# A two-layer SSD and HGRN2 trunk in float32: the SSD layer's TensorE order written out by hand, with one run of 64-wide products a tile, the time steps spread over 128 partitions, products of zeros at the start, another place for the residual's load, and new amounts of background work in HGRN

## The chip, the cores and the metric

The kernel runs on one core of a Trainium2 chip. The metric is the device time of one execution in microseconds (us), the median of several runs. TensorE (PE) multiplies matrices, VectorE (DVE) and ScalarE (ACT) work on elements, GpSimd (POOL) does almost nothing here, and the queue of SyncE (SP) issues all DMA transfers.

## The reference, cut to what matters

One sequence of 512 tokens with 1024 features passes two layers. Layer 0 mixes tokens with Mamba-2 SSD, layer 1 with HGRN2; each is followed by a layer norm, a squared-ReLU MLP, a second norm and a gated embedding. The part that the change rewrites most is the SSD mixer (32 heads of 64 columns in 4 groups, state 128, chunks of 128 tokens):

```python
zxbcdt = u @ w_in
z, xbc, dt = jnp.split(zxbcdt, [SSD_D_INNER, SSD_D_INNER + SSD_CONV_DIM], axis=-1)
xbc = jax.nn.silu(causal_depthwise_conv(xbc, conv_w, conv_b))
...
dt = jax.nn.softplus(dt.astype(jnp.float32) + dt_bias.astype(jnp.float32))
...
xdt = xs * dt[..., None]
a_cs = jnp.cumsum(da, axis=2)
cb = jnp.einsum('bclgn,bcsgn->bcgls', cm, bm)
y_diag = jnp.einsum('bcgls,bcgrls,bcsgrp->bclgrp', cb, decay, xdt)
decay_to_end = jnp.exp(a_cs[:, :, -1:] - a_cs)
states = jnp.einsum('bclgn,bclgr,bclgrp->bcgrpn', bm, decay_to_end, xdt)
...
y_off = jnp.einsum('bclgn,bcgrpn,bclgr->bclgrp', cm, prev, jnp.exp(a_cs))
y = y_diag + y_off + d_skip.astype(jnp.float32).reshape(g_, r_)[:, :, None] * xs
y = y.reshape(bsz, seq, SSD_D_INNER) * jax.nn.silu(z.astype(jnp.float32))
y = rms_norm(y.reshape(bsz, seq, g_, SSD_D_INNER // g_), norm_w.reshape(g_, SSD_D_INNER // g_))
```

## The kernel before, in words

Large products are made of three: both operands are split into a high part and a rest, and `mm3` (L114) multiplies high by high, high by low and low by high (L115 to L117). A weight tile (`unit`, L98) is loaded by SP into one of three `raw` buffers; ACT rounds it to its high part (L109) and DVE subtracts (L111).

**The start.** Eight DMAs bring x and the first four weight tiles together (`slots`, the first four in the memory of the residual `acc`). PE runs eight k-steps of four tiles each, twelve products a step. After step 3 it takes in the dt projection (L499): eight 32-wide products of 512 columns, spread over four groups of rows that DVE adds afterwards (L508, L510). DVE and ACT then work out softplus, the decay and its running sum on 32 partitions of 512 columns (L512 to L541). `dt_tail` turns three results to tokens on partitions. The residual x is loaded into `acc` (L711) when its slots have been read, and scaled (L713).

**SSD.** Tile j of 16 holds a pair of heads. `xz(j)` projects its x and z (24 products each) and runs the convolution (four steps: ACT L557, DVE L560 three times) and silu. `core(j)` transposes x (L619), multiplies by dt and by the weights to the chunk's end, forms three state products (L631), sums them over chunks on DVE (`pv`, L638 to L641), builds the masked decay `m` (L647 to L651), then the eight diagonal products (L661, 64 columns wide, one for each head and chunk) and three off-diagonal ones (L666, 128 wide), whose result DVE multiplies by the decay `ecs` and adds (L674, L675). Every four tiles the group's rms (L691) and output projection follow. The code is written with `core` one tile behind `xz`; the framework's scheduler decides by priorities which engine does what when, so PE's order mixes products of different tiles. PSUM has four banks `pj` for projections and one each for `pt`, `py0`, `py1` and `pm`.

**HGRN.** Here PE's order is written by hand: four pairs of heads pass nine stages, and between stages a generator of background work (the other projections and half of the output projection) is drawn on for an amount of `FILL`, after `AHEAD` at the start. An amount of 0.68 stands for three products of 512 columns. `need` draws on it without counting when a pair's q, f, v or g isn't there yet. The stage `gates` multiplies q by f on DVE (L872 to L874); the next product (L882, 80 columns) reads it. L965 to L969 prepare the operands of L990.

Of the kernel before, what the change touches and what calls it, by code (L numbers as in the profile page):

```python
# [11 lines left out]
AF = mybir.ActivationFunctionType  # L12
# [22 lines left out]
FILL = dict(gates=3.0, first=7.0, fours=5.5, halves=5.0, blocks=4.0, turn=2.7, state=4.0, out=6.7, end=3.0)  # L35
AHEAD = 3.0
# [4 lines left out]
def trunk(ctx: ExitStack, tc, a):  # L41
# [28 lines left out]
    two = dict(xs=2, sz=2, cv=2, cm=2, cbm=2)  # L70
    mlp = dict(r=8, blk=2, sg=2)
    bufs = dict(ssd=dict(two, ss=2), mlp0=mlp, hgrn=dict(qx=2, f=2, k=4, qo=2, qt=2, xc=2, gg=2, tot=2, sc=2, scd=2, btok=2, pv=2), mlp1=mlp)
# [70 lines left out]

    x_s = Split(8)
# [28 lines left out]
    dtc = cols["dtc"][0:32]  # L173
    cmask = tmp("cm", [32, T])
    nc.gpsimd.memset(cmask, 1.0)
    nc.gpsimd.memset(cmask.rearrange("p (c l) -> p c l", c=NCH)[:, :, 0:1], 0.0)
# [318 lines left out]
    for k in range(8):  # L495
        if k == 4:
            for i in range(8):
                r = 32 * (i % 4)
                nc.tensor.matmul(  # L499
                    ps[r : r + 32], dtw[:, 32 * i : 32 * i + 32], slots[i][:, 0, :], start=i < 4, stop=i >= 4  # L500
                )
        for i, out in enumerate(first):
            hi, lo = (v[:, k % 2, i * P : (i + 1) * P] for v in four[k // 2])
            mm3(out, hi, lo, x_s.h(k), x_s.l(k), k == 0, k == 7)
    row = lambda tag: tmp(tag, [32, T])
    dtb, alog = dtc[:, 0:1], dtc[:, 1:2]
    pre = row("pv")
    nc.vector.tensor_copy(pre, ps[0:32])  # L508
    for r in (32, 64, 96):
        nc.vector.tensor_add(pre, ps[r : r + 32], pre)  # L510
# [16 lines left out]
    ea = mk(cpool, [32, 1], "ea")  # L527
# [4 lines left out]
    nc.vector.tensor_tensor_scan(cs, cmask, da, 0.0, ALU.mult, ALU.add)  # L532
    csd = a["csd"]
    nc.sync.dma_start(csd, cs)

    wt = row("sz")
    csv = cs.rearrange("p (c l) -> p c l", c=NCH)
    last_cs = cs.rearrange("p (c l) -> p c l", c=NCH)[:, :, P - 1]
    nc.vector.tensor_sub(wt.rearrange("p (c l) -> p c l", c=NCH), bc(last_cs, 2, P), csv)
    nc.scalar.activation(wt, wt, AF.Exp)  # L540
    nc.vector.tensor_mul(wt, wt, dt)  # L541
    def dt_tail():

        toks = []
        for src, tag in ((dt, "dt_tok"), (wt, "w_tok"), (cs, "cs_tok")):
            pt = bank(pst, "pt")
            for c in range(NCH):
                nc.tensor.transpose(pt[:, c * 32 : (c + 1) * 32], src[:, c * P : (c + 1) * P], ident[:32, :32])
            t = mk(cpool, [P, NCH, 32], tag)
            nc.vector.tensor_copy(t, pt[:, : 4 * 32].rearrange("p (c h) -> p c h", c=NCH))  # L550
            toks.append(t)
        return toks
# [29 lines left out]
    def bc_prep(bcm):  # L582
        bm, cm = bcm
        pt = bank(pst, "pt")
# [4 lines left out]
        pc = bank(psy, "py0")  # L589
# [9 lines left out]
    toks = []  # L599

    def xz(j):
        ps = projected(10 * (j // 4) + 2 + 2 * (j % 4))
        xs = tmp("xs", [P, T])
        conv_silu(ps, j, xs)
        if j == 1:
            toks.extend(dt_tail())
# [3 lines left out]
        return xs, sz  # L610

    def core(j, xs, sz, y, toks, btok, cbm, cm):
        dt_tok, w_tok, cs_tok = toks
# [3 lines left out]
        pt = bank(pst, "pt")  # L617
        for c in range(NCH):
            nc.tensor.transpose(pt[:, c * P : (c + 1) * P], xs[:, c * P : (c + 1) * P], ident)  # L619
        xdt = tmp("xdt", [P, 8, 64])  # L620
        v = pt.rearrange("p (c h q) -> p (c h) q", c=NCH, h=2)
        xdt4 = xdt.rearrange("p (c h) q -> p c h q", c=NCH)
        hs = slice(2 * j, 2 * j + 2)
        ptv = pt.rearrange("p (c h q) -> p c h q", c=NCH, h=2)
        nc.vector.tensor_mul(xdt4, ptv, bc(dt_tok[:, :, hs], 3, 64))
        xw = tmp("xw", [P, 3, 2, 64])
        nc.vector.tensor_mul(xw, ptv[:, 0:3], bc(w_tok[:, 0:3, hs], 3, 64))

        pst_ = bank(psm, "pm")
        for c in range(3):  # L630
            nc.tensor.matmul(  # L631
                pst_[:, c * P : (c + 1) * P], btok[:, c, :], xw[:, c].rearrange("p h q -> p (h q)"), start=True, stop=True
            )
        cd = mk(sm, [P, 2, NCH], "cd")
        nc.scalar.activation(cd, csb.rearrange("p h (c l) -> p h c l", c=NCH)[:, :, :, P - 1], AF.Exp)
        pv = tmp("pv", [P, 3, 2, 64])
        stv = pst_[:, : 3 * P].rearrange("p (c h q) -> p c h q", c=3, h=2)
        nc.vector.tensor_copy(pv[:, 0], stv[:, 0])  # L638
        for c in range(1, 3):
            nc.vector.tensor_mul(pv[:, c], pv[:, c - 1], bc(cd[:, :, c], 2, 64))  # L640
            nc.vector.tensor_add(pv[:, c], stv[:, c], pv[:, c])  # L641

        m = mk(w4, [P, 2, T], "b")
        for r in range(2):
            for c in range(NCH):
# [11 lines left out]
        yd = bank(psy, "py0")  # L657
        for c in range(NCH):
            sl = slice(c * P, (c + 1) * P)
            for r in range(2):  # L660
# [17 lines left out]
    def sq_sum(y, ss):  # L678
        sq = tmp("ss" if ss is None else "sq", [P, T])
        nc.scalar.activation(sq, y, AF.Square)  # L680
        if ss is None:
            return sq
# [524 lines left out]
```

## Time and profile before

| | us |
|---|---|
| median of 3 runs | 1442.93 (1442.82 to 1443.78) |
| the profiled execution | 1443.15 |
| its span on the core | 1441.4 |
| SSD, first real product to first transposition for the norm | 4.85 to 370 |
| first MLP and gate, to HGRN's first 80-column product | 370 to 827 |
| HGRN's head pairs, to the last pair's output transposition | 827 to 1030 |

How to read the rows: a timeline row is start, length, engine, line, operation, output<-inputs, shapes, count, and in brackets the idle time before it with what ended it. Products in float32 (those not from `mm3`) leave two records each, transpositions one. A group's row has the total busy time, the mean in ns of one, and the idle time before.

### The profile page before, as it was taken

What the parts mean: (1) busy time and instruction counts of PE and PEld (TensorE: products, weight loads), DVE (VectorE), ACT (ScalarE), POOL (GpSimd) and SP (SyncE); (2) the same over time, 40 slices, a digit from 0 to 9 for tenths busy, and PEclk for the clock granted to TensorE, in tenths of its full rate; (3) what the DMA queues carried; (4) which work ended last, traced back from release to release, by engine and by line L of the source; (5) the groups of instructions that cost most, each with busy time, mean ns of one, the idle gap of its engine ahead of it and who ended that gap; (6) DMA issues with size and microseconds to landing.
All of it is one profiled execution on the core that took longest, in us unless ns stands there. A gap on an engine that the chain in (4) does not pass through costs nothing.

```text
span 1441.4 us, 20138 instructions
## 1 busy us (share of the span) xinstructions
PE 1422.9 (99%) x7992; PEld 1176.7 (82%) x7992; DVE 1042.7 (72%) x1729; ACT 734.7 (51%) x1080; POOL 1.9 (0%) x11
## 2 busy tenths in 40 slices
PE   8999999999999999999999999999999999999998
PEld 6788888888888888888888887887798888888887
DVE  7999677787966768677863557558795867667873
ACT  5886455554255454535542454645455454544541
POOL 0000000000000000000000000000000000000000
PEclk9999999999999999999999999999999999999999
DMA  6343333323433444443422322222433444444231
GB/s 257 123 139 121 112 109 103 104 100 103 175 117 121 145 135 155 133 149 114 146 89 75 117 89 75 88 89 65 156 118 117 137 142 146 139 139 161 88 118 44
DMA packets 48383, 174.82 MB, mean 121 GB/s; under 512 B 5376, under 2 KB 6016, under 8 KB 48160
## 3 DMA queue, kind: packets, MB, share of 16 engines
q1 hardware_dynamic: 48288, 173.52, 35.9%
q8 instruction: 63, 1.03, 0.3%
q14 instruction: 32, 0.26, 0.1%
HBM read 171.34 MB, written 2.16 MB: 120 GB/s over the span
## 4 chain that ended last, share of the span: by engine, by line
PE 91%; DVE 5%; ACT 2%; DMA 1%; issue 1%; SPq 0%; ACTq 0%
PE pj L115 23%; PE pj L116 23%; PE pj L117 23%; PE py L116 5%; PE py L117 5%; PE py L115 5%; PE py L661 1%; PE pm L631 1%; DVE wlo L111 1%; PE pt L224 1%; PE py L666 1%; DMA raw<-in_wssd 1%; PE pt L619 1%; PE py L882 1%; PE py L1027 0%
## 5 line engine op out<-in xcount | busy, mean ns | idle before, releaser
L109 ACT CAST whi<-raw 128x1024 fp32r<-128x1024 f32 x224 | 234.6, 1051 | 348.3 <-PE pj L116 217.7
L111 DVE TENSOR_TENSOR wlo<-raw,whi 128x1024 fp32r<-128x1024 f32 x224 | 272.0, 1219 | 158.7 <-ACT whi L109 154.3
L115 PE MATMUL pj<-b,whi 128*128 128x512 f32 (+1 forms) x1008 | 382.2, 380 | 0.7 <-ACT b L228 0.7
L116 PE MATMUL pj<-b,whi 128*128 128x512 f32 (+1 forms) x1008 | 381.1, 378 | 0.0
L117 PE MATMUL pj<-b,wlo 128*128 128x512 f32 (+1 forms) x1008 | 380.8, 378 | 0.2 <-DVE wlo L111 0.2
L115 PE MATMUL pj<-whi,b 128*128 128x512 f32 (+1 forms) x584 | 229.5, 393 | 0.7 <-ACT sg L478 0.5
L117 PE MATMUL pj<-whi,b 128*128 128x512 f32 (+1 forms) x592 | 230.0, 389 | 0.0
L116 PE MATMUL pj<-wlo,b 128*128 128x512 f32 (+1 forms) x584 | 227.4, 389 | 0.0
L117 PEld LDWEIGHTS pj<-b,wlo 128*128 128x128 f32 x1008 | 189.7, 188 | 34.7 <-DVE wlo L111 0.6
L116 PEld LDWEIGHTS pj<-b,whi 128*128 128x128 f32 x1008 | 189.9, 188 | 33.4 <-issue 1.0
L115 PEld LDWEIGHTS pj<-b,whi 128*128 128x128 f32 x1008 | 189.5, 188 | 33.4 <-ACT b L228 0.9
L117 PEld LDWEIGHTS pj<-whi,b 128*128 128x128 f32 x592 | 111.3, 188 | 22.4 <-issue 0.2
L115 PEld LDWEIGHTS pj<-whi,b 128*128 128x128 f32 x584 | 109.7, 188 | 23.7 <-ACT b L1068 0.7
L116 PEld LDWEIGHTS pj<-wlo,b 128*128 128x128 f32 x584 | 109.8, 188 | 21.0
L109 ACT CAST whi<-r 128x1024 fp32r<-128x1024 f32 x64 | 67.4, 1053 | 63.7 <-PE pj L117 35.6
L111 DVE TENSOR_TENSOR wlo<-r,whi 128x1024 fp32r<-128x1024 f32 x64 | 78.1, 1220 | 22.6 <-ACT whi L109 22.3
L117 PE MATMUL py<-whi,b 128*128 128x512 f32 x216 | 84.1, 389 | 0.0
L116 PE MATMUL py<-wlo,b 128*128 128x512 f32 x192 | 74.7, 389 | 0.0
L115 PE MATMUL py<-whi,b 128*128 128x512 f32 x192 | 74.4, 389 | 0.0
L560 DVE SCALAR_TENSOR_TENSOR cv<-pj,cst,cv 128x509 f32<-128x509 f32 (+2 forms) x66 | 49.0, 742 | 5.0 <-ACT cv L557 4.5
L117 PEld LDWEIGHTS py<-whi,b 128*128 128x128 f32 x216 | 40.5, 188 | 8.5
L115 PEld LDWEIGHTS py<-whi,b 128*128 128x128 f32 x192 | 36.0, 188 | 7.6
(293 smaller groups left out, 1829.7 us busy)
## 6 DMA issues: line engine op xcount, KB each, us to landing
raw<-in_w SPq DMA_DIRECT2D x112, 512.0 KB, 3.3
r<-in_w SPq DMA_DIRECT2D x64, 512.0 KB, 3.6
raw<-in_wssd SPq DMA_DIRECT2D x36, 512.0 KB, 3.4
a<-csd SPq DMA_DIRECT2D x16, 512.0 KB, 3.8
raw<-in_wso SPq DMA_DIRECT2D x16, 512.0 KB, 3.3
raw<-in_wg SPq DMA_DIRECT2D x16, 512.0 KB, 3.3
raw<-in_whvg SPq DMA_DIRECT2D x16, 512.0 KB, 3.4
raw<-in_whq SPq DMA_DIRECT2D x16, 512.0 KB, 3.3
```

The costliest lines, as they stand in the source:

```text
L109: nc.scalar.copy(hi[:, :n], f)
L111: nc.vector.tensor_sub(lo[:, :n], f, f32(hi[:, :n]))
L115: nc.tensor.matmul(out, sh, mh, start=start, stop=False, **kw)
L116: nc.tensor.matmul(out, sh, ml, start=False, stop=False, **kw)
L117: nc.tensor.matmul(out, sl, mh, start=False, stop=stop, **kw)
L224: nc.tensor.transpose(pt[:, j * P : (j + 1) * P], src[:, k * P : (k + 1) * P], ident)
L560: nc.vector.scalar_tensor_tensor(cv[:, d:], ps[:, : T - d], convw[:, i, k : k + 1], cv[:, d:], ALU.mult, ALU.add)
L619: nc.tensor.transpose(pt[:, c * P : (c + 1) * P], xs[:, c * P : (c + 1) * P], ident)
L631: nc.tensor.matmul(pst_[:, c * P : (c + 1) * P], btok[:, c, :], xw[:, c].rearrange("p h q -> p (h q)"), start=True, stop=True)
L661: nc.tensor.matmul(yd[64 * r : 64 * r + 64, sl], xdt[:, 2 * c + r, :], m[:, r, sl], start=True, stop=True)
L666: nc.tensor.matmul(yo[:, c * P : (c + 1) * P], pv[:, c - 1].rearrange("p h q -> p (h q)"), cm[:, c * P : (c + 1) * P], start=True, stop=True,)
L882: nc.tensor.matmul(ps[r][32 * b : 32 * b + 32, base + n * c : base + n * c + n], kk[r][:, ts], moving(r, 4 * c + b), start=True, stop=True,)
```

## The change

At the start PE multiplies a tile of zeros eight times; in k-step 0 the four high-by-high products stand first, then high weights' rests, then those with the low part of x. The dt projection is cut into 32 products of 128 columns, so that four groups of 32 partitions each hold one chunk; all steps on dt have 128x128 elements, the sum over four groups goes, and three transpositions take the place of twelve.

In SSD, PE's order is written by hand (`manual_schedule`): tile j's x projection, the states of tile j-1, the products of tile j-2, the z projection, the turning of x, and two parts of a finished group's output projection. `ecs` now holds the decay for both heads on all partitions and is multiplied by C before the product, so that the off-diagonal products are 64 wide too and add into the diagonal's bank. The residual's load and scaling stand in the code at tile 4 instead of 0. More buffers are given to seven tiles. In HGRN, `AHEAD` and six amounts change, and eight of the copies of the stage `blocks` move behind the turning of k.

```diff
-FILL = dict(gates=3.0, first=7.0, fours=5.5, halves=5.0, blocks=4.0, turn=2.7, state=4.0, out=6.7, end=3.0)
-AHEAD = 3.0
+FILL = dict(gates=2.0, first=7.0, fours=5.5, halves=4.5, blocks=4.5, turn=2.7, state=3.5, out=6.5, end=2.0)
+AHEAD = 20.0
...
+    zero = tmp("y", [P, P])
+    with tc.high_priority(offset=FIRST + 100):
+        nc.vector.memset(zero, 0.0)
+        rest = bank(psm, "pm")
+        for i in range(8):
+            nc.tensor.matmul(rest[:, 0:P], zero, zero, start=True, stop=True)
...
-                r = 32 * (i % 4)
-                nc.tensor.matmul(
-                    ps[r : r + 32], dtw[:, 32 * i : 32 * i + 32], slots[i][:, 0, :], start=i < 4, stop=i >= 4
-                )
+                for c in range(NCH):
+                    nc.tensor.matmul(
+                        ps[32 * c : 32 * c + 32, 0:P],
+                        dtw[:, 32 * i : 32 * i + 32],
+                        slots[i][:, 0, c * P : (c + 1) * P],
...
+        if k == 0:
+            for out, (hi, lo) in zip(first, parts):
+                nc.tensor.matmul(out, hi, x_s.h(0), start=True, stop=False)
+            for out, (hi, lo) in zip(first, parts):
+                nc.tensor.matmul(out, lo, x_s.h(0), start=False, stop=False)
+            for out, (hi, lo) in zip(first, parts):
+                nc.tensor.matmul(out, hi, x_s.l(0), start=False, stop=False)
...
-    row = lambda tag: tmp(tag, [32, T])
+    row = lambda tag: tmp(tag, [P, P])
...
-        ecs = tmp("ecs", [P, 3 * P])
-        for r in range(2):
-            rs = slice(64 * r, 64 * r + 64)
-            nc.scalar.activation(ecs[rs], csb[rs, r, P:], AF.Exp)
+        ecs = tmp("ecs", [P, 2, 3 * P])
+        nc.scalar.activation(ecs, csb[:, :, P:], AF.Exp)
+        nc.vector.tensor_mul(ecs, ecs, bc(cm[:, P:], 1, 2))
...
+    def mixed(j):
+        xs, sz, xw, xdt, cd, m, ecs, pv = live.pop(j)
+        yd = bank(psy, "py%d" % (j % 2))
+        for c in range(NCH):
+            sl = slice(c * P, (c + 1) * P)
+            for r in range(2):
+                nc.tensor.matmul(yd[64 * r : 64 * r + 64, sl], xdt[:, c, r, :], m[:, r, sl], start=True, stop=c == 0)
+            for r in range(2 if c else 0):
...
+                    pv[:, c - 1, r, :],
+                    ecs[:, r, (c - 1) * P : c * P],
...
+    with tc.manual_schedule(engines={mybir.EngineType.PE}):
+        for j in range(17):
+            if j < 16:
+                load_decay(j)
+                if j % 4 == 0:
+                    bcm[j // 4] = bc_group(j // 4)
+                x_part(j)
...
+            if j == 4:
+                nc.sync.dma_start(acc, a["x"])
+                for c in range(NCH):
+                    nc.vector.tensor_scalar(acc[:, c, :], acc[:, c, :], ALPHA, None, ALU.mult)
...
+            states(j - 1)
+            done = mixed(j - 2)
+            if j % 4 == 2 and j > 2:
+                outs = pieces(j // 4 - 1, rms_group(j // 4 - 1, bank(psy, "py1")))
+            finish(j - 2, *done)
+            if j < 16:
+                z_part(j)
...
+                turn_x(j, bank(pst, "pt"))
+                decays(j)
+                next(outs, None), next(outs, None)
```

What this does to the engines' orders is seen at three places. The first is PE's order around the products of tile 6, before the change:

```order
L115 MATMUL pj_1526<-b_3_100,whi_1529 128x512
L661 MATMUL py_264_1504<-b_1490,xdt_1474 64x128 x4
L631 MATMUL pm_1478<-xw_1476,btok_1048 128x128 x3
L661 MATMUL py_264_1504<-b_1490,xdt_1474 64x128 x4
L116 MATMUL pj_1526<-b_5_102,whi_1529 128x512
L117 MATMUL pj_1526<-b_3_100,wlo_1531 128x512
L115 MATMUL pj_1526<-b_3_100,whi_1529 128x512
L116 MATMUL pj_1526<-b_5_102,whi_1529 128x512
L117 MATMUL pj_1526<-b_3_100,wlo_1531 128x512
L666 MATMUL py_265_1513<-cm_833,pv_1484 128x128
```

and the same tile with the change (L668 are the states of tile 7, L685 the diagonal and L687 the off-diagonal products of tile 6):

```order
L117 MATMUL pj_1558<-b_6_112,wlo_1563 128x512
L668 MATMUL pm_1596<-xw_1432,btok_972 128x128 x3
L685 MATMUL py_272_1606<-b_1267,xdt_1263 64x128 x4
L687 MATMUL py_272_1606<-ecs_1276,pv_1365 64x128 x2
L685 MATMUL py_272_1606<-b_1267,xdt_1263 64x128 x2
L687 MATMUL py_272_1606<-ecs_1276,pv_1365 64x128 x2
L685 MATMUL py_272_1606<-b_1267,xdt_1263 64x128 x2
L687 MATMUL py_272_1606<-ecs_1276,pv_1365 64x128 x2
L115 MATMUL pj_1629<-b_5_111,whi_1632 128x512
```

The eight 64-wide products were cut by the three state products and the off-diagonal ones were strewn among a projection's; now all fourteen of a tile stand together. The second place is DVE's order where the first convolutions begin, before the change (L532 is the running sum of the decay, L713 the scaling of the residual, L560 a convolution step):

```order
L532 SCALAR_TENSOR_TENSOR y_301<-cm_160,xs_299 32x512
L560 SCALAR_TENSOR_TENSOR cv_316<-py_26_169,cst_158,cv_316 128x510
L539 TENSOR_TENSOR sz_304<-y_301 32x512
L560 SCALAR_TENSOR_TENSOR cv_316<-py_26_169,cst_158,cv_316 128x511
L560 SCALAR_TENSOR_TENSOR cv_323<-pj_170,cst_158,cv_323 128x509
L713 TENSOR_SCALAR acc_99<-acc_99 128x1024
L560 SCALAR_TENSOR_TENSOR cv_323<-pj_170,cst_158,cv_323 128x510
L541 TENSOR_TENSOR sz_304<-sz_304,xdt_295 32x512
L560 SCALAR_TENSOR_TENSOR cv_323<-pj_170,cst_158,cv_323 128x511
L713 TENSOR_SCALAR acc_99<-acc_99 128x1024 x2
L111 TENSOR_TENSOR wlo_507<-raw_503,whi_505 128x1024
```

and with the change (L548 is the running sum, L750 the scaling, L572 a convolution step):

```order
L548 SCALAR_TENSOR_TENSOR y_330<-cm_171,xs_328 128x128
L555 TENSOR_TENSOR sz_336<-sz_336,xdt_324 128x128
L750 TENSOR_SCALAR acc_99<-acc_99 128x1024 x4
L111 TENSOR_TENSOR wlo_515<-raw_511,whi_513 128x1024
L572 SCALAR_TENSOR_TENSOR cv_344<-py_27_178,cst_169,cv_344 128x509
L572 SCALAR_TENSOR_TENSOR cv_351<-py_28_179,cst_169,cv_351 128x509
L572 SCALAR_TENSOR_TENSOR cv_344<-py_27_178,cst_169,cv_344 128x510
```

The dt steps and all four scalings now stand ahead of the convolutions; the scheduler has put the residual there although the code has it at tile 4, and SP's order has its load after the first two weight tiles, as before. The third place is DVE's order at the border of two head pairs in HGRN, before the change (L1069 is the last step of pair 1, L872 to L874 the gates of pair 2's second head):

```order
L1069 SCALAR_TENSOR_TENSOR b_1133_6677<-py_1278_7831,cst_158,b_1132_6676 128x512
L1069 SCALAR_TENSOR_TENSOR b_1133_6677<-py_1279_7832,cst_158,b_1132_6676 128x512
L907 TENSOR_TENSOR qo_7941<-qx_7692,f_7779 128x32x4
L918 TENSOR_TENSOR qo_7941<-qo_7941,tot_7943 128x32x8
L937 TENSOR_TENSOR qt_8048<-qo_7941,tot_7943 128x32x4
L919 TENSOR_TENSOR qo_7941<-qo_7941,tot_7943 128x32x4
L938 TENSOR_TENSOR qt_8048<-qo_7941,tot_7943 128x32x8
L111 TENSOR_TENSOR wlo_8309<-raw_8305,whi_8307 128x1024
L872 TENSOR_TENSOR qx_7816<-qx_7816,f_7865 128x32x12
```

and with the change (L926 to L928 are these gates, L1125 pair 1's last step):

```order
L926 TENSOR_TENSOR qx_7761<-qx_7761,f_7830 128x32x12
L963 TENSOR_TENSOR gg_8027<-f_7830 128x128
L927 TENSOR_TENSOR qx_7761<-qx_7761,f_7830 128x32x8
L964 TENSOR_TENSOR gg_8027<-f_7830,gg_8027 128x128
L928 TENSOR_TENSOR qx_7761<-qx_7761,f_7830 128x32x4
L965 TENSOR_TENSOR tot_8012<-f_7830,gg_8027 128x128
L1110 RECIPROCAL hri_7882<-hms_7872 128x8
L1114 SCALAR_TENSOR_TENSOR qo_7856<-pt_7854,hri_7882,b_6667 128x128 x4
L1114 SCALAR_TENSOR_TENSOR qo_7857<-pm_7855,hri_7882,b_6667 128x128 x4
L111 TENSOR_TENSOR wlo_8345<-raw_8341,whi_8343 128x1024
L961 TENSOR_TENSOR qo_8009<-qx_7581,f_7660 128x32x4 x3
L1125 SCALAR_TENSOR_TENSOR b_1124_6796<-py_1272_7927,cst_169,b_1123_6795 128x512
```

The gates of the next pair have moved from behind the previous pair's last step to ahead of its output's scaling.

More of the change, by code (lines that the diff above doesn't have):

```diff
@@ L1019, in heads @@
             nc.scalar.copy(kt[r], pt[r][:, : 3 * P].rearrange("p (c k) -> p c k", c=3))
+        for r in R:
+            for b in range(4):
+                to = slice(32 * b, 32 * b + 32)
+                nc.scalar.copy(full[r][to, :, to], small[r][to])
         yield FILL["turn"]
```

234 lines of the change are left out of this document (119 added, 115 removed).

## The prediction

> **What bounds the kernel now.** I read the page's busy times first, then busy time by windows, then the timeline of single engines.
>
> ```profile
> PE 1422.9 (99%) x7992; PEld 1176.7 (82%) x7992; DVE 1042.7 (72%) x1729; ACT 734.7 (51%) x1080; POOL 1.9 (0%) x11
> ```
> TensorE (PE) is busy 99% of 1441.4 us. The profiled execution took 1443.15 us, so 1.75 us lie outside its span, and it is 0.2 us over the median of 1442.93. A busy PE is not a PE at its peak: the ends of products are modelled and overlap, so I go by start-to-start distances. A gain can only come from fewer or cheaper products, from waits of PE, or from the border between two kinds of products. The windows show where another engine is close behind (columns: span, then busy us and instructions of PE, PEld, DVE, ACT, POOL, then clock, DMA share, GB/s).
>
> ```profile
> 60.00:100.00 40.00, 40.00 (x217) 33.01 (x216) 37.48 (x77) 35.25 (x44) 0.00 (x0) 1.00 0.36 124
> ...
> 140.00:180.00 40.00, 40.00 (x195) 32.82 (x194) 28.46 (x49) 20.64 (x27) 0.00 (x0) 1.00 0.29 99
> ```
> Between 60 and 100 us VectorE (DVE) is nearly full too, 37.5 of 40 us; later in the same SSD stage it has 28.5 of 40. So only at the start can a second engine hold PE up for long.
>
> **The change, part by part.**
>
> *The start: eight products of zeros, and the first k-step in another order.*
>
> ```profile
> 4.85 0.80 PE L115 MATMUL py<-b,whi 128*128 128x512 f32 x1 [4.85 <-ACT b L156]
> 5.99 0.80 PE L116 MATMUL py<-b,whi 128*128 128x512 f32 x1 [0.34 <-DVE b L161]
> ...
> 8.70 0.40 PE L116 MATMUL pj<-b,whi 128*128 128x512 f32 x1
> ...
> 9.85 0.39 PE L115 MATMUL py<-b,whi 128*128 128x512 f32 x1
> ...
> 12.57 0.39 PE L115 MATMUL py<-b,whi 128*128 128x512 f32 x1
> ```
> These are starts of the k-steps 0, 1 and 2, twelve products each, with two products inside step 0. Step 0 takes 5.00 us, step 1 takes 2.72, which is 0.227 a product. The 2.28 us between them are a wait for the low part of x (1.14 us from the first start to the second) and a slow pace: the six starts from 5.99 to 8.70 lie 0.45 apart. If PE already ran at full pace at 4.85, with the four hi x hi products first, so that nothing waits for the low parts, the whole 2.28 us would go. If the pace rises only as late after PE's first work as now (8.70 - 4.85 = 3.85 us) and the zeros start at about 1 us, it rises at about 4.9. If the rise comes later than that, up to seven of the twelve are 0.2 us slower. Bounds 0.9 and 2.3; below zero is excluded, since the zeros end at about 4.2 us, before the first real product at 4.85 (estimate: a product of 128 columns takes 0.2 us at full pace by the L631 rows below, so 0.4 at half pace; eight of them from about 1 us). I take 1.7.
>
> The Trainium skill ("TensorE: Matmul & The Clock Gate", Part 1) says the full clock comes after one busy window of 3.4 us, and that these windows run free of the kernel's start. By that rule the rise falls anywhere from 4.4 to 7.8 us and the term is 0.9 to 2.3; the trace has one rise, at about 8.7, and cannot tell where a window lies.
>
> *Runs of 64-wide products.* Each of the 16 head pairs issues eight 64-wide products (L661, 16 records). Rows of whole and of cut runs:
>
> ```profile
> 101.03 0.83 PE L631 MATMUL pm<-xw,btok 128*128 128x128 f32 x6
> 101.62 0.48 PE L116 MATMUL pj<-b,whi 128*128 128x512 f32 x1
> ...
> 104.56 1.09 PE L661 MATMUL py<-b,xdt 128*64 128x128 f32 x16
> 105.59 0.50 PE L117 MATMUL pj<-b,wlo 128*128 128x512 f32 x1
> ...
> 167.59 0.66 PE L661 MATMUL py<-b,xdt 128*64 128x128 f32 x8
> 168.18 0.94 PE L631 MATMUL pm<-xw,btok 128*128 128x128 f32 x6
> 169.05 0.66 PE L661 MATMUL py<-b,xdt 128*64 128x128 f32 x8
> 169.63 0.50 PE L116 MATMUL pj<-b,whi 128*128 128x512 f32 x1
> ```
> Whole run 1.03 us and the three state products alone 0.59 with 0.08 on the next start: 1.70. Cut by the state products the same work takes 169.63 - 167.59 = 2.04, so a cut costs 0.34. The order of before shows 12 cut runs (pairs 4 to 15), that of the change none: 12 x 0.34 = 4.1 us. Three of the four rms products now join such a run and save one border of that size each: 1.0 us. The off-diagonal products change from three 128-wide (0.59 to 0.67, as L631) to six 64-wide: 12 records at (1.03 - 0.59)/8 = 0.055 are 0.66, so nothing, provided that accumulating pairs overlap as L661's do. Sum **5.1 us**, all on PE and so on the path.
>
> *Decay rows, and time steps on 128 partitions.* Multiplying the decay into C before the product removes two DVE operations of 384 columns per pair and adds one of 768: with 1.13 us for 1024 columns (below) 0.85 to 0.95 against about 1.0. Nothing. The dt chain goes from 32x512 to 128x128:
>
> ```profile
> 25.65 3.33 DVE L521 RECIPROCAL cbm<-cv 32x512 f32<-32x512 f32 x1
> ...
> 42.16 0.73 DVE L560 SCALAR_TENSOR_TENSOR cv<-pj,cst,cv 128x511 f32<-128x511 f32 x1
> 42.82 1.27 DVE L713 TENSOR_SCALAR acc<-acc 128x1024 f32<-128x1024 f32 x2
> 44.02 1.20 DVE L111 TENSOR_TENSOR wlo<-raw,whi 128x1024 fp32r<-128x1024 f32 x1
> 45.15 0.73 DVE L560 SCALAR_TENSOR_TENSOR cv<-pj,cst,cv 128x509 f32<-128x509 f32 x1
> ```
> A quarter of the columns makes the reciprocal some 0.85 us and the other ten about 0.25, where they were 0.4 to 1.2; the chain then ends before the first convolution instead of among its steps. ScalarE (ACT) gets nine more table loads by the order; with 20.6 of 40 us busy from 140 on they lie beside PE's work, though between 60 and 100 ACT has 35.3 of 40 and is the next engine that could be late. Start to start these rows give DVE's real cost: 0.66 us for a convolution step, 0.60 for a residual scaling, 1.13 for a weight split.
>
> *The residual is not later.* The order shows the x load at the same place of SP's queue and all four L750 in one block ahead of the third split and every convolution. It can start when the dt products have read the slots that it overwrites.
>
> ```profile
> 19.30 0.33 SPq L711 DMA_DIRECT2D acc<-in_x  x1
> ```
> ```profile
> acc<-in_x SPq DMA_DIRECT2D x1, 2048.0 KB, 8.7
> ```
> Now issued at 19.30 and 8.7 us long; with the start 1.7 us sooner about 17.6, landing at 26.3, scaled by 28.7. DVE then starts on the split at about 28.9.
>
> *The hand order against a full DVE.* PE may no longer run ahead: the state products of pair 1 write the one bank pm that pair 0's state sums (pv) still read. From 28.9 to the last of those sums DVE's order holds 7 splits (7.9 us), 15 convolution steps (9.9), 16 of L653, the old L647:
>
> ```profile
> L647 DVE TENSOR_SCALAR b<-a,cs_tok 128x128 f32<-128x128 f32 x128 | 31.3, 277 | 0.0
> ```
> at 0.21 start to start, 0.07 less than the mean as for the other rows (3.4), four 1024- or 768-wide multiplications of two pairs (4.1), the xw/xdt products, tokens and mask (3.2) and five sums (1.0): 29.5 us, done at **58.4**. PE's own work to the same point starts where the first four tiles end:
>
> ```profile
> 31.01 0.39 PE L115 MATMUL pj<-b,whi 128*128 128x512 f32 x1
> ...
> 74.37 0.48 PE L115 MATMUL pj<-b,whi 128*128 128x512 f32 x1
> ```
> 31.01 less the start's 1.7 is 29.3; then come four weight tiles of 24 products (21.8), the preparation of group 0 with its transpositions and the first two pairs' (2.4), and the states of pair 0 (0.7): 54.2. So PE **waits 4.2 us**, in one or two places. After that come, in us of PE, states 0.7, the run of pair 0 1.9 (28 records with both borders), a turn 0.4, a tile 5.5, states 0.7, the run of pair 1 1.9, a tile 5.5 and a turn 0.4: 75.4.
>
> The kernel before stands at 74.37 (the second row) with the same tiles and runs, but one turn and one set of states less, so at 75.5 for equal work. The start's gain is thus **eaten**: 0.1 us left. Behind this point a group's B and C tiles (10.9 us of PE) let DVE catch up, and each pair's product operands are two pairs old, so I cost waits there at nothing; their cover is a z tile, 5.5 us, against some 4 us of convolution and silu.
>
> *HGRN.* The background starts 20 us ahead instead of 3, so the q and f of pairs 1 to 3 are ready before their gates, and the gates move in DVE's order ahead of the previous pair's output.
>
> ```profile
> 827.06 1.31 PE L882 MATMUL py<-qx,k 128*32 128x80 f32 x64
> 828.30 0.50 PE L115 MATMUL pj<-whi,b 128*128 128x512 f32 x1
> ...
> 878.61 0.76 PE L882 MATMUL py<-qx,k 128*32 128x80 f32 x32
> 881.05 0.76 PE L882 MATMUL py<-qx,k 128*32 128x80 f32 x32 [1.68 <-DVE qx L874]
> ```
> 64 records take 1.24 us at pair 0; at pair 1 the second half starts 2.44 after the first instead of 0.62: 1.82 lost, and likewise at 937 and 993: **5.5 us**. Given back: the background ends sooner, so the last pair has 11 products (2.5 us) instead of 21 ahead of its L1044.
>
> ```profile
> 1011.22 0.28 DVE L969 TENSOR_TENSOR xc<-xc,tot 128x128 f32<-128x128 f32 x1
> ```
> The last operand of that product was ready at 1011.50; 21 products of 0.238 ran ahead of its start at 1013.22, so they began at 1008.22, and the operand took 3.3 us. With 2.5 us of cover 0.8 are missing. Net **4.7 us** (bounds 1.5, if all 4 us less of cover are missed, and 5.5).
>
> **Sum:** 0.1 + 5.1 + 4.7 = 9.9 us off 1443.15: **1433.2 us**.
>
> **Rivals.**
> 1. *DVE does not hold PE up at the start* (its operations overlap more, or the x load lands sooner). For it: the wait is a difference of two sums of 25 to 30 us. Against: 37.5 of 40 busy. The 4.2 us stay: 1429.0.
> 2. *Covers too thin:* HGRN keeps 1.5 instead of 4.7, and the early wait is 2 us longer. For it: five FILL amounts shrink, and the last pair waited already. 1438.4.
> 3. *The 64-wide accumulating products do not overlap in pairs.* Then each costs what a 128-wide one does: 6 x 0.22 instead of 0.66, 0.66 more in each of 16 pairs, 10.6 us: 1443.8, no change. Against: L661 overlaps in the same halves of the bank; no accumulating 64-wide pair is in the trace.
> 4. *Slower:* the single bank pm. If DVE's queue reaches the state sums late in every later pair and not only in the first, each states(j-1) waits. From 0.75 us a pair (9.9 us over 13 pairs) nothing is gained; at 1.1 us the time is 1447.5. Against: from 140 to 180 us DVE has 28.5 us of work in 40, so it catches up by 11.5 us in two pairs.
>
> **How the numbers follow.** Forecast (1430.5 to 1436) 0.50; rival 1 0.18; rival 2 0.17; rival 3 0.06; rival 4 0.07; 0.02 for no gain from other causes. A measurement of this kernel tells 0.2%, 2.9 us, from no change. Faster: 0.50 + 0.18 + 0.17 = 0.85; same 0.08; slower 0.07. The range takes in the forecast and rivals 1 and 2, with the start's and the transitions' bounds: 1427 to 1440.
>
> **What would show it.** First full-pace product by 6 us, k-step 1 at about 8.2. A PE wait near 42 to 59 us of some 4 us, ended by DVE (pv sums) or ACT (silu). Each pair's 64-wide run in one piece of about 1.75 us. No wait of the 80-column products on qx; a wait of about 0.8 us at L1044 in the last pair. Wrong would be the forecast if PE waits in every pair, if the runs take over 2.2 us, or if the first wait is missing.

## The result, and the profile after

| | median | runs | against before (95%) |
|---|---|---|---|
| before | 1443.36 us | 1442.82 to 1445.11 | |
| changed | 1431.63 us | 1430.75 to 1435.61 | 0.9922 (0.9901 to 0.9943) |
| forecast | 1433.2 us | 1427 to 1440 | |

The change takes 11.7 us off, where 9.9 were forecast. The profiled execution of the changed kernel is the slowest of its four, 1435.61 us; what sets it apart from the others (1430.75 to 1431.97) is one of the findings below.

First the same rows as before, of the changed kernel: the page's busy times, and busy time by windows (span, busy us and instructions of PE, PEld, DVE, ACT, POOL, then granted clock, DMA share, GB/s).

```profile
PE 1419.9 (99%) x8143; PEld 1183.8 (83%) x8143; DVE 1032.0 (72%) x1707; ACT 742.4 (52%) x1073; POOL 1.6 (0%) x10
```
```profile
60.00:100.00 40.00, 40.00 (x238) 33.57 (x238) 32.70 (x65) 23.69 (x30) 0.00 (x0) 0.94 0.34 114
```
PE is as full as before, and VectorE has 32.7 us of work in this window instead of 37.5. New is the clock of 0.94.

Next PE's timeline at four places that can be found in both kernels (start, busy us, line, tiles): behind the turn of pair 2, at the first and the last transpositions of the first norm, and at the first of the second. Of the changed kernel:

```profile
78.83 0.48 PE L115 MATMUL pj<-b,whi 128*128 128x512 f32 x1
...
365.81 0.60 PE L230 MATMUL pt<-cst,acc 128*128 128x128 f32 x4
...
392.93 0.65 PE L230 MATMUL pt<-cst,acc 128*128 128x128 f32 x4 [0.69 <-DVE b L235]
...
1029.99 0.60 PE L230 MATMUL pt<-cst,acc 128*128 128x128 f32 x4
```
In the kernel before, the norms' transpositions (there L224) stand at 369.98, 398.13 and 1039.13. With 75.5 as the place of equal work before (the prediction's figure), the difference of the spans, 1433.8 against 1441.4, falls into stages:

| stage | before | after | measured | forecast |
|---|---|---|---|---|
| start to the turn of pair 2 | 75.5 | 78.8 | +3.3 | -0.1 |
| the rest of SSD | 294.5 | 287.0 | -7.5 | -5.1 |
| first norm | 28.2 | 27.1 | -1.0 | 0 |
| MLP and HGRN | 641.0 | 637.1 | -3.9 | -4.7 |
| second norm to the end | 402.3 | 403.8 | +1.5 | 0 |

The first row and the last are worse than forecast, the rest in sum better.

**The early wait.** PE's timeline of the changed kernel at the states of pair 1, with what ended the idle time in brackets, and DVE's in the same place:

```profile
55.96 0.39 PE L117 MATMUL pj<-b,wlo 128*128 128x512 f32 x1
59.14 1.62 PE L668 MATMUL pm<-xw,btok 128*128 128x128 f32 x6 [2.79 <-DVE pv L676]
60.69 1.12 PE L685 MATMUL py<-b,xdt 128*64 128x128 f32 x8
...
70.45 0.83 PE L668 MATMUL pm<-xw,btok 128*128 128x128 f32 x6
71.21 0.66 PE L685 MATMUL py<-b,xdt 128*64 128x128 f32 x8
```
```profile
54.91 1.22 DVE L111 TENSOR_TENSOR wlo<-raw,whi 128x1024 fp32r<-128x1024 f32 x1
56.05 0.28 DVE L676 TENSOR_TENSOR pv<-pm,pv 128x128 f32<-128x128 f32 x1
56.25 1.21 DVE L111 TENSOR_TENSOR wlo<-raw,whi 128x1024 fp32r<-128x1024 f32 x1
57.38 0.28 DVE L675 TENSOR_TENSOR pv<-pv,cd 128x128 f32<-128x128 f32 x1
57.58 1.21 DVE L111 TENSOR_TENSOR wlo<-raw,whi 128x1024 fp32r<-128x1024 f32 x1
58.72 0.28 DVE L676 TENSOR_TENSOR pv<-pm,pv 128x128 f32<-128x128 f32 x1
```
The last state sum of pair 0 ends at 59.00; the forecast had 58.4. Three weight splits stand between the sums. PE has nothing to do from 56.2 to 59.1, and had lost 1.3 us near 42 us at the first transpositions. Then the same products take twice as long as later: the states of pair 1 need 1.55 us to the next start, those of pair 2 0.76. The windows show the granted clock there:

```profile
58.00:65.00 7.00, 5.86 (x39) 5.34 (x40) 4.62 (x10) 2.90 (x5) 0.00 (x0) 0.52 0.81 261
65.00:73.00 8.00, 8.00 (x59) 6.69 (x59) 7.65 (x16) 4.03 (x5) 0.00 (x0) 0.99 0.22 75
```
By windows of half a microsecond the clock is halved from 58.3 to 65.1 us, some 6.8 us: it falls while PE still waits, and stays down for 6 us of its work. From the states of pair 1 to 78.83 it took 19.7 us, where a kernel without the wait takes 16.8 (55.17 to 71.95 in the kernel with another bank, below): the spell costs 2.9 us.

**The last pair of HGRN and the second norm.** What PE waited for between 800 and 1070 us (us in all, times, longest), before and after:

```profile
PE py L882 <- DVE qx L874: 4.9, 3, 1.7
PE pt L1018 <- DVE k L999: 1.4, 1, 1.4
```
```profile
PE pt L230 <- DVE b L235: 1.5, 2, 1.2
PE py L1044 <- DVE scd L1026: 1.2, 1, 1.2
PE py L1083 <- ACT btok L1071: 0.6, 2, 0.4
```
The waits at the gates are gone, and L1044 waits in the last pair, as forecast. The wait at the second norm (L230) is new. It comes from one weight load, as ScalarE's timeline there shows:

```profile
1044.20 1.05 ACT L109 CAST whi<-raw 128x1024 fp32r<-128x1024 f32 x1 [4.70 <-DMA raw<-in_w]
```
ScalarE stands at the cast of a weight that has not landed, and the norm's own cast L234 queues behind it. Of the ten later profiles of kernels with the new HGRN amounts nine lose at most 0.2 us there, and one, that of the kernel with another bank below, 1.5 us behind the same late load (4.78 us). So the late load comes in some executions of a kernel and not in others; whether the change makes it more frequent is not shown.

### The profile page after: what moved, and what is told of

It reads as the page before. It is cut to its first block, busy times and chain, and to the rows that moved or that the text cites. A ratio compares the mean times of both kernels' runs of the same rounds, so it can differ in the third digit from the quotient of the medians.

```text
span 1433.8 us, 20405 instructions
## 1 busy us (share of the span) xinstructions
PE 1419.9 (99%) x8143; PEld 1183.8 (83%) x8143; DVE 1032.0 (72%) x1707; ACT 742.4 (52%) x1073; POOL 1.6 (0%) x10
## 3 DMA queue, kind: packets, MB, share of 16 engines
q8 instruction: 64, 1.05, 0.3%
## 4 chain that ended last, share of the span: by engine, by line
PE 92%; DVE 4%; ACT 2%; DMA 1%; issue 0%; ACTq 0%; DVEq 0%
PE pj L115 24%; PE pj L116 24%; PE pj L117 23%; PE py L117 5%; PE py L115 5%; PE py L116 5%; PE py L685 1%; DVE wlo L111 1%; PE pt L230 1%; PE py L687 1%; PE pm L668 1%; DMA raw<-in_wssd 1%; PE py L936 1%; PE pt L634 1%; PE py L1083 0%; ACT whi L109 0%
## 5 line engine op out<-in xcount | busy, mean ns | idle before, releaser
L572 DVE SCALAR_TENSOR_TENSOR cv<-pj,cst,cv 128x509 f32<-128x509 f32 (+2 forms) x66 | 48.6, 742 | 8.7 <-ACT cv L569 8.4
```

What stands on the lines that cost most here:

```text
L572: nc.vector.scalar_tensor_tensor(cv[:, d:], ps[:, : T - d], convw[:, i, k : k + 1], cv[:, d:], ALU.mult, ALU.add)
```

## The experiments

Each run was timed against runs of the kernel before on the same chip, whose medians were 1444.19 to 1444.25 us.

### The changed kernel again

No edit.

> The changed kernel once more, unaltered. In the profile of the changed kernel (1435.61 us, the other executions 1430.75 to 1431.97) PE waits 3.0 us until 59.1 us, and from 58.3 to 65 us the granted clock is 0.5. Theory: the half clock follows the wait and comes in some executions only; it costs 3.3 us. Then a profile without it has the states of pair 1 in 0.76 us instead of 1.55 and a time of 1431 to 1432, one with it about 1435.5; the wait of 3.0 us is there in both. Rival: the half clock is in every execution and the 4 us come from elsewhere, the 1.5 us of wait at the second norm among them (there a weight load took 5.0 us, in the kernel before 3.6): then the spell shows again with a time near 1431. Median by both 1431.6.

Measured: median 1432.59 us (1433.9, 1431.43, 1431.6, 1433.58), ratio 0.9919 (0.9905 to 0.9933). The profile, of the run of 1433.9 us, shows the wait of 2.79 us again (the states of pair 1 start at 58.75) and the spell of half clock with it:

```profile
58.00:65.00 7.00, 6.25 (x40) 5.63 (x41) 4.59 (x11) 2.50 (x5) 0.00 (x0) 0.51 0.79 252
```
and the mean clocks of the four executions are 0.997, 0.998, 1.0 and 0.997. With the four of the first result, executions with a clock of 1.0 took 1430.75 to 1431.6 us and those below it 1431.43 to 1435.61. So the half clock comes in some executions, as the theory had it. The late load at the second norm is absent, which is most of the 1.7 us between the two profiled runs.

### Work in the place of the wait

```diff
+hold = bank(psy, "py0")
+[nc.tensor.matmul(hold[:, 0:P], ident, ident, start=True, stop=True) for _ in range(12)]
 states(1)
```


> Twelve products of the 128x128 identity with itself (0.224 us each, 2.7 us in all, into bank py0, which nobody reads) stand ahead of the states of pair 1, in the place of the 3.0 us wait. Theory: the wait itself stays, since DVE's sums end it, but PE is at work in it, so the clock stays at 1.00 in the profile; the time is 1431 to 1432 in every execution, with no 1435. Rival: the lower clock has nothing to do with the wait, and shows here as often as in the kernel without these products. If the wait were shorter than 2.7 us the products would add to the time.

Measured: 1430.99 us (1429.84 to 1431.27), ratio 0.9906 (0.9893 to 0.992); the clock is 0.999 or 1.0 in all four executions. In the profile the states of pair 1 start as late as without the products, and at full pace (L763 are the products put in):

```profile
56.02 2.84 PE L763 MATMUL py<-cst 128*128 128x128 f32 x24
58.96 0.91 PE L668 MATMUL pm<-xw,btok 128*128 128x128 f32 x6
```
DVE's sums still set the place, the half clock goes, and so do the times above 1431.3. The lower clock is thus a consequence of PE's idleness, so far as four executions show it (a mean of 0.999 can still hide a short spell, as a profile below does). The Trainium skill ("TensorE: Matmul & The Clock Gate", Part 1) says that the clock goes down after an idle window of about 3.4 us, and that the windows run free of the kernel. That it hits only some executions agrees; that it takes 3.4 us of idleness does not, since here 2.8 us by the row were enough, and 1.9 in a run below.

### Another bank for the states of pair 1

```diff
-                states(1)
+                states(1, bank(psy, "py1"))
```


> The state products of pair 1 write another bank (py1), which is free by then. Theory: they wait for the one bank pm only. PE then goes on at 56.1 us with the states of pair 1 (0.76 us) and with the run of pair 0 up to its last off-diagonal products, which need the last state sum of pair 0 (done at 59.0); of 3.0 us of wait about 0.6 remain, in front of the last L687, the clock stays at 1.00, and the time falls by 2.4 us to 1429.2. Rival: the state sums themselves, not the bank, hold PE up: it waits as long in the run of pair 0, and the time stays at 1431.6.

Measured: 1428.13 us (1426.99 to 1428.81), ratio 0.9887 (0.9874 to 0.9901): this beats both kernels, and all its four executions are below all eight of the changed kernel. PE's timeline where the wait was, and DVE's:

```profile
55.17 0.83 PE L668 MATMUL py<-xw,btok 128*128 128x128 f32 x6
...
57.28 0.39 PE L687 MATMUL py<-ecs,pv 128*64 128x128 f32 x4
```
```profile
56.64 0.29 DVE L676 TENSOR_TENSOR pv<-pm,pv 128x128 f32<-128x128 f32 x1
...
57.04 1.22 DVE L111 TENSOR_TENSOR wlo<-raw,whi 128x1024 fp32r<-128x1024 f32 x1
```
No wait is left, where 0.6 us were expected, because the last sum of pair 0 is done at 56.93 instead of 59.00: in this profile the start was 0.9 us sooner, and DVE's order changed with the bank: one weight split, not three, now stands between the sums, and another behind them. The gain over the changed kernel's median in the same comparison is 4.5 us, the wait and the spells. It was the bank, and the order that follows from it, not the sums' data: PE needs the last of them only at 57.28. How much each of the two is worth was not parted.

### The residual really later

```diff
             if j == 4:
+                nc.vector.tensor_copy(acc[:, 0, 0:1], live[2][-1][:, 0, 0, 0:1])
                 nc.sync.dma_start(acc, a["x"])
```


> The load of the residual x is made to wait for the state sums of pair 2 (one column of them is first copied into acc), so that the load and its four scalings L750 really come later, after 72 us instead of at 18 and 26.7 us. Theory: DVE's queue before the state sums of pair 0 sets the early wait; four scalings of 0.60 us leave it, the sums are done at 56.6 instead of 59.0, the wait at the states of pair 1 falls from 3.0 to about 0.6 us, the clock stays at 1.00, and the time is 1429.2. Rival: DVE waits elsewhere for the same time (for the decay loads, which now queue behind three more weight loads, or for ACT), and the time stays within 1 us of 1431.6; or the load collides with weight loads after 72 us and gives new waits of some us there.

Measured: 1429.49 us (1429.39 to 1433.57), ratio 0.9908 (0.9895 to 0.9922): three executions at 1429.4 to 1429.5 with a clock of 1.0, and 1431.8 and 1433.57 with 0.998. The profile, of one of the three:

```profile
PE pm L668 <- DVE pv L676: 1.2, 1, 1.2
PE pt L634 <- ACT btok L599: 1.1, 1, 1.1
```
The wait at the states falls from 2.8 to 1.2 us; part is handed to the transpositions (0.7 in the changed kernel). Three of five executions are where the theory put them. Even this shorter wait leaves two with a lower mean clock, though no profile shows where in them it fell.

### Bank and later residual together

> Both together: the states of pair 1 in bank py1, and the load of x with its scalings held until the state sums of pair 2. Theory: the bank alone left no wait at the states of pair 1, so the four scalings are off the path there, and what is left to gain are the waits of the first transpositions near 42 us (1.0 us): 1427 to 1428.1, no difference that the runs can tell. Rival: the gains of the two add up (2.4 each): 1426.

Measured: 1430.52 us (1429.79 to 1432.42), ratio 0.9904 (0.9891 to 0.9918). Both expectations missed: it is 2.4 us slower than the bank alone. PE's longest wait between 38 and 66 us, SP's queue (start of the first issue, us, line, count) and DVE's running sum, of this kernel, and then SP's queue with the bank alone:

```profile
PE pt L634 <- ACT btok L599: 2.4, 1, 2.4
```
```profile
7.80 19.51 SPq L102 DMA_DIRECT2D raw<-in_wssd  x7
27.71 1.73 SPq L551 DMA_DIRECT2D csd<-y  x4
```
```profile
27.26 0.42 DVE L548 TENSOR_TENSOR_SCAN y<-cm,xs 128x128 f32<-128x128 f32 x1
```
```profile
18.12 0.33 SPq L102 DMA_DIRECT2D raw<-in_wssd  x1
23.94 1.73 SPq L551 DMA_DIRECT2D csd<-y  x4
```
With the load of x gone from the front, seven weight loads go ahead of the store of the decay rows, instead of three, and it starts at 27.7 instead of 23.9 us. What it waits for last is not the queue but its data, the running sum, which ends at 27.68 (23.92 with the bank alone): the casts and splits of the weights that landed sooner stand inside ScalarE's and DVE's work on dt. ScalarE then waits 1.5 us for the decay rows, and its copy of btok, on which PE's transpositions wait, stands behind them. The run before had named late decay rows as a rival. There the store was as late (27.48), and the rows, asked for at the same time (31.2 and 31.1 us), kept ScalarE for 0.3 us only. This profile is of the slowest of four executions, so part of the 2.4 us is a late landing; how much the order alone costs was not parted.

### Without the zeros, in both kernels

The memset and the eight products are left out.

> The changed kernel without the eight products of zeros; k-step 0 keeps its new order. Theory: the zeros alone raise PE's pace sooner, so that step 1 starts later again, at about 9.9 us instead of 8.72 (twelve products 0.43 apart from 4.8 us on); but the states of pair 1 wait for DVE's sums, so of the 1.1 us nothing is left at that point: PE waits 1.9 us instead of 3.0, the sums are done at 59.0 as before, and the time stays at 1431.6 to 1432.6 with the same spread. Rival: DVE is pulled later with PE, since its convolutions read PE's first tiles; then the sums come 1.1 us later too and the time is 1432.7 to 1433.7.

Measured: 1432.82 us (1432.65 to 1433.99), ratio 0.9923 (0.9911 to 0.9936). PE at the states of pair 1:

```profile
59.09 1.29 PE L668 MATMUL pm<-xw,btok 128*128 128x128 f32 x6 [1.92 <-DVE pv L676]
```

> The kernel with the states of pair 1 in bank py1 (1428.1 us), without the eight products of zeros. There the wait at the states of pair 1 is gone, so by the theory that this wait eats the start's gain the loss of 1.1 us at the start now reaches the end: about 1429.2. Rival: the transpositions of the first two pairs, which wait 0.3 and 0.9 us near 42 us in every profile of the changed kernel for ScalarE and VectorE, eat it as well; then the time stays at 1428.1.

Measured: 1431.77 us (1430.89 to 1433.74), ratio 0.9914 (0.99 to 0.9927), 3.6 us over the same kernel with zeros. PE's first product and k-step 1 (it starts at 10.10), then PE at the first transpositions, and k-step 1 of the kernel with zeros:

```profile
4.81 1.22 PE L516 MATMUL py<-b,whi 128*128 128x512 f32 x2 [4.81 <-ACT b L163]
...
10.52 0.63 PE L116 MATMUL py<-b,whi 128*128 128x512 f32 x1
10.95 0.43 PE L117 MATMUL py<-b,wlo 128*128 128x512 f32 x1
...
47.58 0.66 PE L634 MATMUL pt<-cst,xs 128*128 128x128 f32 x4 [2.83 <-ACT btok L599]
```
```profile
7.85 0.39 PE L115 MATMUL py<-b,whi 128*128 128x512 f32 x1
```
Without zeros the full pace came at 8.3 us in the one profile and at 10.95 in the other; in the eleven with zeros it came between the first product (4.7) and 7.3. In the kernel that still waits, the states of pair 1 start at 59.09 against 59.14 and 58.75 with the zeros: the loss of the start (0.5 us in this profile, with step 1 at 9.24) does not arrive there, as the theory had it, and the medians lie 0.2 to 1.2 us apart. In the kernel with the other bank the loss arrives, and is 3.6 us instead of 1.1. Its profile, of the slowest of five executions, starts step 1 later by 2.25 us. There x is issued at 19.96 instead of 17.24 us, since its place is free only when the dt products have run, and it takes 9.5 instead of 7.6 us to land; its scalings start at 29.4 instead of 24.9, DVE's convolutions behind them, and PE then waits 2.8 us at the transpositions, until 47.6 us, with a half clock from 48.6 on. The other four executions have a mean clock of 1.0 and took 1430.89 to 1432.55 us, so the loss is there without the half clock too; their early waits were not seen.

### The old order of the first k-step

> The kernel with the states of pair 1 in bank py1 (1428.1 us), with the products of k-step 0 in the old order (three products a tile), the zeros kept. Theory: the second product then waits for the low part of x, as in the profile of before, where it started 1.14 us after the first; step 1 starts 0.6 to 0.9 us later than the 7.85 to 8.72 us of the profiles with the new order, and the time is 1428.7 to 1429.2. Rival: the low part is ready while PE is still at half pace, so that nothing is lost: 1428.1.

Measured: 1427.6 us (1427.03 to 1427.93), ratio 0.9883 (0.9868 to 0.9898): no loss. But PE's timeline shows that this was no test of the old order:

```profile
4.74 0.73 PE L115 MATMUL py<-b,whi 128*128 128x512 f32 x2
5.31 0.63 PE L115 MATMUL pj<-b,whi 128*128 128x512 f32 x2
```
The scheduler put the four hi x hi products first by itself. What the run shows is that the rest of the hand order (all lo products, then all products with the low part of x) brings nothing that these four executions show; what the old order would cost beside the zeros stays open.

### A cut in the 64-wide run

```diff
 nc.tensor.matmul(yd[...], xdt[:, c, r, :], m[:, r, sl], start=True, stop=c == 0)
+if mid and (c, r) == (1, 1): mid()
...
-            states(j - 1)
-            done = mixed(j - 2)
+            done = mixed(j - 2, lambda: states(j - 1))
```


> The kernel with the states of pair 1 in bank py1 (1428.1 us), with the state products of pair j-1 inside the 64-wide run of pair j-2, after four of its products, in the 14 pairs from j=3 on. Theory: a cut after a pair of products costs 0.33 us, as where the kernel before cut its run after four of eight (2.24 us with the borders against 1.9 uncut): 14 x 0.33 = 4.6 us, 1432.7. Rival: what made the runs cheaper is not the missing cut but the off-diagonal products that no longer stand alone; then the cut costs under 1 us in all.

With (1, 0) the cut falls one product earlier:

> The same with the cut after three products, that is between the two halves of a pair of 64-wide products, as in pairs of the kernel before that ran 3 + 5 or 5 + 3 (2.35 us and 0.10 on either side). Theory: a cut there costs 0.2 us more than one after four, 0.54 in all, because two 64-wide products that would overlap are parted: 14 x 0.54 = 7.6 us, 1435.7. Rival: every cut costs the same 0.33 and both kernels take 1432.7.

Measured: even 1431.82 us (1431.16 to 1432.84), ratio 0.9916 (0.9902 to 0.9929); odd 1434.98 us (1434.77 to 1436.31), ratio 0.9939 (0.9926 to 0.9951). A pair in one piece in the changed kernel, then one with the even cut, from PE's timelines:

```profile
95.05 0.39 PE L117 MATMUL pj<-b,wlo 128*128 128x512 f32 x1
95.27 0.83 PE L668 MATMUL pm<-xw,btok 128*128 128x128 f32 x6
...
96.52 0.39 PE L687 MATMUL py<-ecs,pv 128*64 128x128 f32 x4
96.74 0.39 PE L685 MATMUL py<-b,xdt 128*64 128x128 f32 x4
...
98.05 0.40 PE L116 MATMUL pj<-b,whi 128*128 128x512 f32 x1
```
```profile
105.07 0.39 PE L117 MATMUL pj<-b,wlo 128*128 128x512 f32 x1
105.39 0.66 PE L685 MATMUL py<-b,xdt 128*64 128x128 f32 x8
105.98 0.94 PE L668 MATMUL pm<-xw,btok 128*128 128x128 f32 x6
...
108.42 0.39 PE L116 MATMUL pj<-b,whi 128*128 128x512 f32 x1
```
From the last dense product before the pair to the second behind it, 3.00 us uncut and 3.35 with the even cut; the same count for the odd one (105.04 to 108.60) gives 3.56. A cut costs 0.35 after an even number of products and 0.56 after an odd one. Over 14 pairs that is 4.9 and 7.8 us; the medians are 3.7 and 6.9 over 1428.13, less by about 1 us in both, but apart by 3.2 where 2.9 is due. In the profiles the first norm begins 5.6 and 8.2 us later than in that of the kernel with the bank alone (358.93), so there nothing is missing; where the medians lose their 1 us no profile shows.

### HGRN's amounts

```diff
-FILL = dict(gates=2.0, first=7.0, fours=5.5, halves=4.5, ...)
-AHEAD = 20.0
+FILL = dict(gates=3.0, first=7.0, fours=5.5, halves=5.0, ...)
+AHEAD = 3.0
```


> The kernel with the states of pair 1 in bank py1 (1428.1 us), with the FILL amounts and the AHEAD of 3 of the kernel before in HGRN. Theory: the new numbers take away the waits of the 80-column products on qx at the gates of pairs 1 to 3 (1.7 to 1.9 us each in the profile of before); they come back, +5.5, and the waits of 1.4 and 0.4 us that the last pair has at L1044 in the profile of the changed kernel go, -1.3: 4.2 us in all, 1432.3. Rival: the gates stay ready, because their place in DVE's order, ahead of the previous pair's output, comes from the moved copies and not from the numbers; then 1427 to 1428.

Measured: 1431.91 us (1431.26 to 1432.63), ratio 0.9912 (0.9898 to 0.9925), 3.8 us over the kernel with the new amounts. The waits of PE at the gates are those of the kernel before, and so is the wait of 1.4 us of the last pair. Counted as in the table of stages, MLP and HGRN take 641.0 us in this profile, as in the kernel before, and 637.1 in that with the new amounts:

```profile
PE py L936 <- DVE qx L928: 4.9, 3, 1.7
```
Then AHEAD alone:

> The same with AHEAD alone put back from 20 to 3, with the new FILL amounts. Theory: the head start alone makes q and f of pairs 1 to 3 ready before their gates, so the three waits come back as with the old FILL, and FILL is worth nothing by itself: 1432 to 1433. Rival: the FILL amounts (less cover at gates and end) are what removed the waits; then the time stays within 1 us of 1428.1.

Measured: 1433.59 us (1432.03 to 1434.07), ratio 0.9921 (0.9909 to 0.9934).

```profile
PE py L936 <- DVE qx L928: 6.4, 3, 3.1
```
It is the head start that takes the waits away: the new FILL amounts without it make them longer (the longest 3.1 us), and three of the five executions have a mean clock of 0.998. The stage takes 641.5 us here. The moved copies are in both kernels and do not remove these waits. The head start with the old FILL was not run.

## Why the prediction was right, point by point

**The start.** Step 1 begins at 8.72 us in the changed kernel's profile, 1.13 sooner than the 9.85 of before; 1.7 was taken, with bounds of 0.9 and 2.3. Over the profiles with zeros it varies from 7.6 to 8.7. The zeros run from 1.05 us right up to the first real product at 4.76; the estimate had them done at 4.2. The full pace follows PE's first work (the zeros at 1.05, else the first product at 4.8) by 3.7 to 6.3 us with the zeros, and by 3.5 to 6.1 in the three profiles without. By the rule of the Trainium skill that the prediction weighed ("TensorE: Matmul & The Clock Gate", Part 1: one busy window of 3.4 us, free-running) it would be 3.4 to 6.8 us, an estimate from that figure, and the runs agree. The full pace by 6 us that the prediction asked for came in some profiles only.

**The early wait.** Place, cause and size are right: 4.3 us in two places (3.0 at the states of pair 1, 1.3 at the first transpositions) against 4.2; the sums ended at 59.0 against 58.4; the four scalings stood ahead of the convolutions as the order showed, ending at 29.2 against 28.7. Rival 1 is out, and so is rival 2, which had this wait 2 us longer and only 1.5 us left of HGRN's gain. "The start's gain is thus eaten" holds where that wait exists. What failed is what the prediction left out: it took a wait of PE for its length alone. With it the clock falls to half in some executions, which cost 2.9 us in the profiled one. That is why its first stage reads +3.3 instead of -0.1: without the 2.9 us it would be +0.4. Where that wait is absent, the start's price reaches the end and more, since x's load hangs on the start; the prediction did not say so.

**The 64-wide runs.** The mechanism is right and the size was too small: 7.5 us against 5.1. The cut was priced by one row, a cut after four of eight products, at 0.34; the runs confirm it, at 0.35. But seven of the cuts in PE's timeline of before fall at odd places, where the price is 0.56: 1.5 us more. The off-diagonal products were taken as an even trade; less the dense products, an uncut pair of before costs 2.61 us with all its borders (states 0.68, run 1.23, three off-diagonal products of 0.23 to 0.24) and one of the changed kernel 2.55, some 0.8 us over 14 pairs. The turns give nothing that can be told: one alone costs 0.45 us in both. Rival 3 is out: the accumulating products overlap at 0.055 us a record (0.22 for four, from 96.52 to 96.74 above). Rival 4 is out as well: from pair 2 on no states wait for the bank; it decides in one pair only.

**HGRN.** The three waits went, and the last pair handed some back: 3.9 us in the profile and 3.8 by the run with the old amounts, against 4.7. The 0.8 us missing at L1044 were 1.2, and 0.6 more are lost at L1083, which the prediction did not name. Nor did it name the wait of 1.4 us of the last pair at L1018, which went as well. By these rows PE waited 6.3 us before and 1.8 after; why 3.9 us came of it and not 4.5 no row here shows.

**The first norm.** 1.0 us less than before, in this profile and, within 0.05 us, in all the others. The prediction had nothing there. Between the last two transpositions of before, PE waits 0.7 us for a cast of ScalarE (L228), and in the changed kernel it does not; that is most of it. What took this wait away no run took apart, and it stays open.

In sum, SSD and the first norm gave 3.4 us more than forecast, HGRN and the start 1.3 less (0.8 and 0.5). That the sum came so near the forecast is in part luck, since these errors go against each other and the norm was not in it. The clock moves single executions of the changed kernel by up to 3 us, and their median by about 1.

## What to carry to other kernels

A wait of PE can have two prices, its own length and what the clock does after it. Here the second came in some executions only, so it showed as spread before it showed in a median, and work put into the hole, or another bank, removed it in the four executions of each. When an accumulator bank is reused by the very next step of a hand order, look at what the reader's engine does between its reads: here three weight splits stood between the sums that kept the bank. And price a cut by where it falls: a run of half-width products that overlap in pairs lost more here when it was cut inside a pair (0.56 us against 0.35).

## What the runs showed of the hardware

- The half clock came in pieces of two lengths: 6.8 us in the two profiles of the changed kernel, and 3.4 in the two without zeros. The stretch of the one with the shared bank, by windows:

```profile
59.50:63.00 3.50, 3.50 (x31) 3.27 (x31) 1.74 (x5) 3.28 (x5) 0.00 (x0) 0.52 0.74 273
```
- It came with waits of 1.9 us (that kernel) and 2.8 us (the other three), by the idle time in PE's rows. It did not come with every wait of that size: the profile of bank and later residual together, with 2.4 us, has none.
- The granted clock in the rows does not show the slow start: in the profile of before it reads 1.00 from 4 to 9 us, where the products start 0.43 us apart, and 0.23 later. That pace has to be read from the starts.
- With a 2 MB load gone from the front of SP's queue, four more weight loads went ahead of a small store; their casts and splits stood in the work that makes its data, and it came 3.8 us later.
